# Two tiles for the weight sums of a seven-product pair, in a decoder-layer kernel

## The chip, the core and the metric

The kernel runs on one core of one Trainium2 chip, alone. Its time is the device time of one execution in microseconds, taken as the median of several executions. A profiled execution also has a span, from the start of the first instruction of the program to the end of the last.

## What is computed

One layer of a decoder with two token mixers, in float32, for 512 prompt tokens and 32 sample tokens that share the weights. Cut to the lines that lead to the weight products:

```python
h = rmsnorm(x, w['norm1']) * (1 + sc1) + sh1
bg, cg, xin, q, kc, vc, ks, vs, kw, vw, nsa_g, merge_g = split_columns(h @ w['w_in'])
v, conv_new = short_conv(cg * xin, conv_prev, w['w_conv'], w['b_conv'])
y_a = (bg * v) @ w['w_out_conv']
o_b, nsa_state = attend(qh, gates, kvh(kc, vc), kvh(ks, vs), kvh(kw, vw))
x = x + g1 * ((ga * y_a + gb * (o_b @ w['w_o_nsa'])) @ w['w_out'])
h2 = rmsnorm(x, w['norm2']) * (1 + sc2) + sh2
x = x + g2 * ((jax.nn.silu(h2 @ w['w_gate']) * (h2 @ w['w_up'])) @ w['w_down'])
```

The input projection `h @ w['w_in']` has 7,728 columns. It gives keys, values, queries, the convolution's inputs and the gates, and it is the part of the program in which the change acts.

## The kernel before, in words

**Stages.** The program runs through compressing the cached keys (lines 640 to 780), the norm and the modulation that make `h`, the input projection (lines 870 to 995), the sample group's attention beside the first part of the convolution (from line 997), the prompt's attention, the output projections, the feed-forward part (from line 1667), and the last norm. All loops are written out, and a list scheduler orders each engine's instructions when the kernel is built. On the chip each engine takes its own instructions strictly in that order, and waits at an instruction until the semaphores that it needs have come.

**A pair and its seven products.** Most of the input projection is done by `seven` (line 284). It takes 256 output columns, a "pair" of 128-column blocks, and cuts the 1,024 input rows into two halves, so that the weights are four blocks. With sums of weight blocks and sums of blocks of `h` (the tiles `S1` to `S4`), seven block products do the work of eight. The weights of a pair arrive in one tile `raw` (128 x 2048, 1 MB) as four blocks `raw[0]` to `raw[3]`. Four sums are wanted, each 128 x 512, all made by VectorE with `tensor_add`. Written with y and z for the sums, they are y1 = raw[0]+raw[3], y2 = y1+raw[1], z1 = raw[1]+raw[0], z2 = y2+raw[2].

**Operands.** A product wants its weights as two float32r tiles: ScalarE copies them into a high part (`to_hilo`, line 410, tiles `wh` or `Wh`), and VectorE subtracts that from the weights for the low part (line 411, tiles `wl` or `Wl`). Four such splits are made for each pair: W0 of raw[1:3], WY of the y sums, WZ of the z sums (128 x 1024 each), and W3 of raw[3] (128 x 512). W0 and WZ go to `wh` and `wl`, WY and W3 to `Wh` and `Wl`; each name has two buffers. A product is 12 matmuls (lines 252 to 254), so a pair is 84.

**Order inside a pair** (`wpair`, line 351). TensorE does W0's first product into `wA` and its second into `wB`, then two with WY (into `wA` and into a third accumulator `wC`), two with WZ (`wA` and `wC`), one with W3 (`wA`). After some of them ScalarE takes a copy of the accumulator, `snap` (line 301), before TensorE may go on adding into it. The outputs are put together by VectorE (`out`, lines 907 and 909) and ScalarE (line 911). The last two products of a pair come after the first one of the next pair.

**Tiles before.** y1 is written over raw[0] (line 335) and y2 over raw[1] (line 337), so WY is split from `raw`, and y2 must wait until W0's split has read raw[1]. z1 (line 334) and z2 (line 343) go to a tile `ws`, of which there are three buffers, one for each pair. `raw` has three buffers too, and the last reader of a pair's `raw` is the split W3; when it is done, SyncE starts the load for the pair three further on (line 238).

**Where pairs occur.** In the input projection there are 23 pairs, in the order of `keys`: keys and values, three of the convolution, queries, three more of the convolution, and the gates. All of them have their sums made by VectorE alone. In the feed-forward part there are 28 pairs, which are "summed": while the input projection runs, `presum` (line 558) has DMAs form y1 and z1 in DRAM, and for such a pair y1 is loaded into raw[0] and z1 into `ws` (lines 317 to 319), so VectorE makes only y2 and z2.

**Names in the profile.** The groups `ws<-raw` at line 334, `raw<-raw` at lines 335 and 337 and `ws<-raw` at line 343 are the sums. `Wl<-raw` at line 411 is WY or W3, `wl<-raw` is W0, `wl<-ws` is WZ.

Of the kernel before, what the change touches and what calls it, by code (L numbers as in the profile page):

```python
# [10 lines left out]
F32 = mybir.dt.float32  # L11
# [145 lines left out]
def build(tc, a, o):  # L157
    nc = tc.nc
    sync, act, dve, pool, pe = nc.sync, nc.scalar, nc.vector, nc.gpsimd, nc.tensor
# [14 lines left out]
    def lin_ps(nm):  # L174
        return ps.tile([128, 512], F32, tag="g", bufs=5, name=nm)
# [4 lines left out]
    def s_ps(nm):  # L180
        return ps.tile([128, 512], F32, tag="sc", bufs=2, name=nm)
# [6 lines left out]
    def nm(s):  # L188
        uid[0] += 1
        return f"{s}_{uid[0]}"  # L190
# [25 lines left out]
    def raw_tile(n):  # L216
        return wpool.tile([128, 2048], F32, tag="raw", bufs=3, name=nm(n))
# [5 lines left out]
    def queue(f, ins=lambda r: r):  # L223

        if not ordered[0]:
            return f()
        if last_q[0] is None:
            r = f()
        else:
            with tc.issue_after(last_q[0].ins):  # L230
                r = f()
        last_q[0] = ins(r)
        return r

    def slab(*key):
        nk, ncol = len(SLABS[key][1]), SLABS[key][2].shape[-1]
        v = raw_tile("raw")[:, 0:nk * ncol]
        last_slab[0] = queue(lambda: sync.dma_start(v, a["wt"][SLAB_AT[key], :, 0:nk * ncol]))
        return v.rearrange("p (k f) -> p k f", k=nk)
# [11 lines left out]
    def mm3(p, wh, wl, xh, xl, k, start, stop, **kw):  # L251
        pe.matmul(p, lhsT=wh[:, k, :], rhs=xh, start=start, stop=False, **kw)  # L252
        pe.matmul(p, lhsT=wh[:, k, :], rhs=xl, start=False, stop=False, **kw)  # L253
        pe.matmul(p, lhsT=wl[:, k, :], rhs=xh, start=False, stop=stop, **kw)  # L254
# [29 lines left out]
    def seven(o_, ww, wlp, wsp):  # L284
        wi, ns, late, later = [0], [0], [iter(())], []
        hooks = iter(o_.splits)

        def wsplit(view, odd=None):
            nk = view.shape[1]
            if odd is None:  # L290
                wi[0] += 1
                odd = wi[0] % 2
            pools = ((wpool, "wh"), (wpool, "wl")) if odd else ((ww, "Wh"), (wlp, "Wl"))
            wh, wl = (p_.tile([128, 8, 128], F32R, tag=t, bufs=2, name=nm(t))[:, 0:nk, :] for p_, t in pools)
            to_hilo(view, wh, wl)
            return wh, wl

        def snap(p):
            t = o_.snaps[ns[0] % 4]
            ns[0] += 1  # L300
            o_.snap_ops.append(act.activation(t, p, AF.Copy))  # L301
            return t

        def product(p, w, k0, X, first):
            n_ = len(X[0]) if isinstance(X[0], list) else 4
            xk = lambda t, k: t[k] if isinstance(t, list) else t[:, k, :]
            k0 *= n_
            for k in range(n_):
                mm3(p, w[0][:, k0:k0 + n_], w[1][:, k0:k0 + n_], xk(X[0], k), xk(X[1], k), k, first and k == 0, k == n_ - 1, skip_group_check=not first)

        def wslab(*key):
            n_ = len(SLABS[key][1]) // 4
            w_ = 128 * n_
            z = wsp.tile([128, 8, 128], F32, tag="ws", bufs=3, name=nm("ws"))[:, 0:2 * n_]
            if key in pre:
                v = raw_tile("raw")[:, 0:4 * w_]
                last_slab[0] = queue(lambda: sync.dma_start(v[:, w_:4 * w_], a["wt"][SLAB_AT[key], :, w_:4 * w_]))
                sync.dma_start(v[:, 0:w_], pre[key][:, w_:2 * w_])
                sync.dma_start(z[:, 0:n_].rearrange("p k f -> p (k f)"), pre[key][:, 0:w_])
            else:  # L320
                v = slab(*key).rearrange("p k f -> p (k f)")
            return v.rearrange("p (n k f) -> p n k f", n=4, k=n_), z, key in pre

        def parts(slabs):
            raw, z, summed = slabs
            n_ = raw.shape[2]
            pair = lambda i: raw[:, i:i + 2].rearrange("p n k f -> p (n k) f")
            return raw, z[:, 0:n_], z[:, n_:2 * n_], pair, summed

        def y_sums(slabs, tie=None):  # L330
            raw, z1, z2, pair, summed = parts(slabs)
            a21, a11, a12, a22 = (raw[:, i] for i in range(4))
            if not summed:
                dve.tensor_add(z1, a11, a21)
                dve.tensor_add(a21, a21, a22)
            with tc.issue_after(tie.ins) if tie else ExitStack():
                dve.tensor_add(a11, a21, a11)
            return wsplit(pair(0))

        def z_sums(slabs, tie=None):  # L340
            raw, z1, z2, pair, summed = parts(slabs)
            with tc.issue_after(tie.ins) if tie else ExitStack():
                dve.tensor_add(z2, raw[:, 1], raw[:, 2])

        def prepare(slabs):
            W0 = wsplit(parts(slabs)[3](1))
            WY = y_sums(slabs)
            z_sums(slabs)
            return W0, WY

        def wpair(slabs, out, ready=None, o_=o_, tie=None):

            W0 = wsplit(parts(slabs)[3](1)) if ready is None else ready[0]
            yield
            pA = s_ps(nm("wA"))[:, 0:WH]
            product(pA, W0, 0, o_.B11, True)
            s1 = snap(pA)
            next(late[0], None)
            pB = lin_ps(nm("wB"))[:, 0:WH]
            product(pB, W0, 1, o_.B21, True)  # L360
            out(0, 0, pB, s1)
            yield
            if ready is None:
                WY = y_sums(slabs, tie)
                z_sums(slabs, tie)
            else:
                WY = ready[1]
            WZ = wsplit(slabs[1])
            W3 = wsplit(slabs[0][:, 3])
            yield  # L370
            product(pA, WY, 1, o_.T2, False)
            s2 = snap(pA)
            for _ in late[0]:
                pass
            next(hooks, lambda: None)()
            pC = lin_ps(nm("wC"))[:, 0:WH]
            product(pC, WY, 0, o_.T1, True)
            s3 = snap(pC)
            next(hooks, lambda: None)()
            flush()  # L380
            product(pA, WZ, 0, o_.T3, False)
            out(1, 1, pA, s3)
            flush()
            next(hooks, lambda: None)()

            def rest():
                product(pC, WZ, 1, o_.B22, False)
                out(0, 1, pC, s2)
                yield
                product(pA, W3, 0, o_.T4, False)  # L390
                out(1, 0, pA, None)
                yield
            late[0] = rest()
            yield

        def flush():
            while later:
                later.pop(0)()

        def finish():  # L400
            for _ in late[0]:
                pass
            flush()
        return SimpleNamespace(wsplit=wsplit, wslab=wslab, wpair=wpair, finish=finish, later=later, prepare=prepare)

    def hcols(hf):
        return slice(*HS[hf])

    def to_hilo(src, hi, lo):
        act.activation(hi, src, AF.Copy)  # L410
        return dve.tensor_sub(lo, src, hi.bitcast(F32))  # L411
# [143 lines left out]
    pre, pre_keys, copied = {}, [(n, c2) for c2 in range(1, FC // 2) for n in ("fg", "fu")], []  # L555
# [326 lines left out]
    ready = h7.prepare(first[0])  # L882
# [682 lines left out]
    for k2 in range(4):  # L1565
# [3 lines left out]
        for kk in range(2):  # L1569
            k = k2 * 2 + kk  # L1570
# [31 lines left out]
    ws = []  # L1602
# [23 lines left out]
    for k2 in range(4):  # L1626
# [3 lines left out]
        for kk in range(2):  # L1630
            v = so[:, :, kk * 128:(kk + 1) * 128]
# [112 lines left out]
    wsplit, wslab, wpair, later = f7.wsplit, f7.wslab, f7.wpair, f7.later  # L1744
# [339 lines left out]
```

## Time and profile before

| what | value |
|---|---|
| median of 3 runs | 1204.36 us (1201.5 to 1205.96) |
| time of the profiled execution | 1200.79 us |
| its span | 1199.0 us, 1.8 us less than its time |
| TensorE (matmuls), busy | 1179.7 us, 98% |
| TensorE (weight loads), busy | 1094.4 us, 91% |
| VectorE, busy | 851.2 us, 71% |
| ScalarE, busy | 640.2 us, 53% |
| HBM traffic over the span | 235 GB/s |
| granted TensorE clock | 0.998 |

The profile is of one execution. PE is TensorE at its matmuls and PEld its weight loads, which run beside them; DVE is VectorE, ACT is ScalarE, POOL is GpSimd, SP is SyncE. A row of the timeline gives start, duration, engine, line, operation, the tile written and the tiles read, and in square brackets how long the engine was idle just before and what ended it. A row of the waits gives the engine and tile that waited, what it waited for, the total, how often, and the longest. The end of a matmul is modelled, and matmuls overlap: each is shown with some 0.29 us, while the next starts 0.13 us later. So a pause of TensorE is shorter as PE idle time than it is as time lost.

### The profile page before, as it was taken

The numbers are of one execution on the slowest core, as the hardware profiler recorded it, in microseconds if no ns is written. First come the engines' busy times: TensorE is split into PE (matmuls) and PEld (weight loads), VectorE is DVE, ScalarE is ACT, GpSimd is POOL, SyncE is SP. The second block draws the span as 40 slices with busy tenths as digits, with TensorE's granted clock in tenths as the row PEclk, the third lists the DMA queues.
The fourth block names the chain that finished last, engine by engine and source line by source line (L and its number), as shares of the span: only waits on it lengthen the run. The fifth ranks groups of instructions, "written<-read, shape, count | busy, mean of one in ns | idle before, by whom it ended". The sixth has DMA issues, their size and how long they took to land.

```text
span 1199.0 us, 25796 instructions
## 1 busy us (share of the span) xinstructions
PE 1179.7 (98%) x10114; PEld 1094.4 (91%) x10114; DVE 851.2 (71%) x1927; ACT 640.2 (53%) x1302; POOL 103.3 (9%) x154
## 2 busy tenths in 40 slices
PE   9999999999999999999999999999999999999997
PEld 7999999999999988887777778999999999999996
DVE  2539976788676477685777766667847887877776
ACT  1416544565446333386666675436645666666541
POOL 1000241000000111111101100000010001001000
PEclk9999999999999999999999999999999999999999
DMA  9963556788655998979978869545357448349412
GB/s 334 358 233 124 154 167 195 215 264 252 192 172 180 381 337 313 308 225 250 275 203 222 218 187 292 175 183 175 96 132 216 128 132 232 134 119 224 172 54 75
DMA packets 86283, 248.81 MB, mean 208 GB/s; under 512 B 9480, under 2 KB 19592, under 8 KB 74522
## 3 DMA queue, kind: packets, MB, share of 16 engines
q1 hardware_dynamic: 73330, 222.77, 53.6%
q0 software_dynamic: 12112, 23.09, 12.2%
q8 instruction: 79, 1.29, 0.4%
q10 hardware_dynamic: 720, 1.31, 0.3%
q14 instruction: 42, 0.34, 0.1%
HBM read 216.33 MB, written 65.28 MB: 235 GB/s over the span
## 4 chain that ended last, share of the span: by engine, by line
PE 76%; DMA 10%; DVE 9%; issue 2%; ACT 1%; ACTq 0%; SPq 0%; DVEq 0%; POOL 0%; POOLq 0%
DMA raw<-in_wt 8%; PE phi L674 7%; PE lin L252 7%; PE lin L253 6%; PE lin L254 6%; PE wA L254 5%; PE wA L252 5%; PE wA L253 5%; PE acc L1464 3%; PE ptp L1470 3%; PE wC L252 3%; DVE wl L411 3%; PE wC L253 3%; PE wC L254 3%; PE modp L430 2%
## 5 line engine op out<-in xcount | busy, mean ns | idle before, releaser
L410 ACT ACTIVATE Wh<-raw 128x1024 fp32r<-128x1024 f32 (+3 forms) x105 | 86.3, 823 | 78.2 <-PE wA L253 35.8
L411 DVE TENSOR_TENSOR Wl<-raw,Wh 128x1024 fp32r<-128x1024 f32 (+3 forms) x105 | 98.3, 940 | 20.3 <-ACT Wh L410 19.9
L1443 ACT ACTIVATE P<-P,nms 128x384 f32<-128x384 f32 (+3 forms) x120 | 64.9, 544 | 20.0 <-DVE nms L1442 19.3
L1442 DVE CUSTOM_DVE_ANT_0 P<-sp,ta 128x384 f32<-128x384 f32 (+3 forms) x120 | 52.1, 469 | 30.2 <-PE sp L1430 22.7
L252 PE MATMUL lin<-h_h,wh 128*128 128x288 f32 (+1 forms) x240 | 71.5, 298 | 0.0
L410 ACT ACTIVATE wh<-ws 128x1024 fp32r<-128x1024 f32 (+1 forms) x50 | 51.3, 1026 | 36.7 <-PE wC L253 20.5
L301 ACT ACTIVATE work<-wA 128x272 f32<-128x272 f32 x102 | 40.0, 392 | 56.3 <-PE wA L254 56.2
L253 PE MATMUL lin<-h_l,wh 128*128 128x288 f32 (+1 forms) x240 | 69.3, 289 | 0.0
L254 PE MATMUL lin<-h_h,wl 128*128 128x288 f32 (+1 forms) x240 | 69.1, 288 | 0.0
L411 DVE TENSOR_TENSOR wl<-raw,wh 128x1024 fp32r<-128x1024 f32 (+2 forms) x56 | 65.1, 1163 | 4.4 <-ACT wh L410 4.0
L411 DVE TENSOR_TENSOR wl<-ws,wh 128x1024 fp32r<-128x1024 f32 (+1 forms) x50 | 59.8, 1197 | 11.0 <-ACT wh L410 9.9
L247 ACT ACTIVATE wh<-raw 128x1024 fp32r<-128x1024 f32 (+1 forms) x43 | 41.9, 974 | 42.3 <-PE lin L253 25.8
L248 DVE TENSOR_TENSOR wl<-raw,wh 128x1024 fp32r<-128x1024 f32 (+1 forms) x43 | 48.3, 1123 | 21.5 <-ACT wh L247 21.3
L410 ACT ACTIVATE wh<-raw 128x1024 fp32r<-128x1024 f32 (+2 forms) x56 | 55.9, 999 | 11.5 <-PE wB L253 4.9
L674 PE MATMUL phi<-gt,wphi 128*128 128x128 f32 x512 | 61.4, 277 | 0.2 <-DMA gt<-in_cache_cmp 0.2
L674 PEld LDWEIGHTS phi<-gt,wphi 128*128 128x128 f32 x512 | 59.1, 192 | 2.4 <-issue 1.1
L573 POOL DMA_DIRECT2D pre<-in_wt x28 | 27.3, 975 | 358.4 <-DMA pre<-in_wt 358.4
L254 PE MATMUL wA<-S_hi,Wl 128*128 128x272 f32 x184 | 53.4, 290 | 1.4 <-DVE Wl L411 1.4
L252 PE MATMUL wA<-S_hi,Wh 128*128 128x272 f32 x184 | 53.4, 290 | 0.0
L253 PE MATMUL wA<-S_lo,Wh 128*128 128x272 f32 x184 | 53.1, 288 | 0.0
L252 PEld LDWEIGHTS lin<-h_h,wh 128*128 128x128 f32 x240 | 45.6, 190 | 7.5 <-issue 6.2
L665 DVE TENSOR_TENSOR xs<-gt 128x1024 f32<-128x1024 f32 x16 | 19.5, 1222 | 36.6 <-PE phi L674 20.5
(584 smaller groups left out, 4336.6 us busy)
## 6 DMA issues: line engine op xcount, KB each, us to landing
raw<-in_wt SPq DMA_DIRECT2D x68, 1024.0 KB, 6.9
raw<-in_wt SPq DMA_DIRECT2D x24, 768.0 KB, 4.8
sraw<-in_cache_sel SPq DMA_DIRECT2D x64, 256.0 KB, 5.9
gt<-in_cache_cmp SPq DMA_DIRECT2D x60, 256.0 KB, 5.7
pre<-in_wt SPq DMA_DIRECT2D x20, 512.0 KB, 8.2
pre<-in_wt POOLq DMA_DIRECT2D x20, 512.0 KB, 7.9
wraw<-in_cache_winT SPq DMA_DIRECT2D x8, 1024.0 KB, 7.9
raw<-pre SPq DMA_DIRECT2D x20, 256.0 KB, 7.4
```

Of the source, the lines that this page charges most:

```text
L247: act.activation(oh, view, AF.Copy)
L248: dve.tensor_sub(ol, view, oh.bitcast(F32))
L252: pe.matmul(p, lhsT=wh[:, k, :], rhs=xh, start=start, stop=False, **kw)
L253: pe.matmul(p, lhsT=wh[:, k, :], rhs=xl, start=False, stop=False, **kw)
L254: pe.matmul(p, lhsT=wl[:, k, :], rhs=xh, start=False, stop=stop, **kw)
L301: o_.snap_ops.append(act.activation(t, p, AF.Copy))
L410: act.activation(hi, src, AF.Copy)
L411: return dve.tensor_sub(lo, src, hi.bitcast(F32))
L674: pe.matmul(po[:, c0:c0 + 128], lhsT=w[:, ch], rhs=x[:, :, ch * 16:ch * 16 + 16], start=(n_ == 0 and ch == 0), stop=(n_ == 2 and ch == 7))
L1442: p_ops.append(dve.tensor_tensor_reduce(out=t[:, 0:n], in0=sps[br], in1=t_dist[:, 512 - n:512], scale=-hs, scalar=3e38, op0=ALU.add, op1=A ...
L1443: e_ops.append(act.activation(t[:, 0:n], t[:, 0:n], AF.Exp, scale=-1.0, bias=nms[:, c:c + 1], accum_out=sums[:, c:c + 1]))
L1464: pe.matmul(acc[br * 64:br * 64 + 64, :], lhsT=vtok[br][:, j, g * 64:(g + 1) * 64], rhs=pts_[br], start=(j == 0), stop=False)
```

## The change

For pairs whose sums VectorE makes alone, `wslab` now takes two `ws` tiles, one for y and one for z. y1 and y2 go to the first, z1 and z2 to the second, and `raw` is only read. z1 is made after WY's split is written in the program, not before. For summed pairs y stays in `raw` and z in `ws`, as before. `ws` still has three buffers, of which one unsummed pair now uses two.

```diff
             if key in pre:
+                z = sums()
                 v = raw_tile("raw")[:, 0:4 * w_]
+                y = v[:, 0:2 * w_].rearrange("p (k f) -> p k f", k=2 * n_)
...
             else:
+                y, z = sums(), sums()
                 v = slab(*key).rearrange("p k f -> p (k f)")
...
-        def y_sums(slabs, tie=None):
-            raw, z1, z2, pair, summed = parts(slabs)
-            a21, a11, a12, a22 = (raw[:, i] for i in range(4))
             if not summed:
-                dve.tensor_add(z1, a11, a21)
-                dve.tensor_add(a21, a21, a22)
+                dve.tensor_add(y[:, 0:n_], raw[:, 0], raw[:, 3])
             with tc.issue_after(tie.ins) if tie else ExitStack():
-                dve.tensor_add(a11, a21, a11)
-            return wsplit(pair(0))
+                dve.tensor_add(y[:, n_:2 * n_], y[:, 0:n_], raw[:, 1])
+            return wsplit(y)

         def z_sums(slabs, tie=None):
-            raw, z1, z2, pair, summed = parts(slabs)
+            raw, y, z, summed = slabs
+            n_ = raw.shape[2]
+            if not summed:
+                dve.tensor_add(z[:, 0:n_], raw[:, 1], raw[:, 0])
             with tc.issue_after(tie.ins) if tie else ExitStack():
-                dve.tensor_add(z2, raw[:, 1], raw[:, 2])
+                dve.tensor_add(z[:, n_:2 * n_], y[:, n_:2 * n_], raw[:, 2])
```

The new lines: y1 is line 334, y2 line 336, z1 line 343, z2 line 345. Everything below the functions moves down by two lines: the splits are at 412 and 413, the outputs at 909, 911 and 913. Each tile has a number that differs between the two programs.

VectorE in the eighteenth of the 23 pairs, which stands for all from the fourth on. Before, raw_451 is pair 17, raw_464 pair 18 and raw_478 pair 19 (the first is pair 0); ws_450 and ws_463 hold the z sums of 17 and 18.

```order
L334 TENSOR_TENSOR ws_477_4012<-raw_478_4013 128x512
L411 TENSOR_TENSOR wl_460_3883<-ws_450_3771,wh_459_3882 128x1024
L907 TENSOR_TENSOR work7_1595<-wB_456_3860,work7_1595 128x272
L411 TENSOR_TENSOR wl_466_3894<-raw_464_3891,wh_465_3893 128x1024
L335 TENSOR_TENSOR raw_478_4013<-raw_478_4013 128x512
L337 TENSOR_TENSOR raw_464_3891<-raw_464_3891 128x512
L411 TENSOR_TENSOR Wl_462_3887<-raw_451_3772,Wh_461_3886 128x512
L343 TENSOR_TENSOR ws_463_3890<-raw_464_3891 128x512
L411 TENSOR_TENSOR Wl_472_4000<-raw_464_3891,Wh_471_3999 128x1024
L909 SCALAR_TENSOR_TENSOR work7_1595<-wA_455_3833,work7_1595 128x272
L907 TENSOR_TENSOR work7_1595<-wC_467_3923,work7_1595 128x272
```

The same place after. raw_469, raw_483 and raw_498 are pairs 17, 18 and 19; ws_468 is the z tile of 17, ws_481 the y tile of 18, ws_496 and ws_497 the y and z tiles of 19.

```order
L413 TENSOR_TENSOR wl_478_3901<-ws_468_3789,wh_477_3900 128x1024
L909 TENSOR_TENSOR work7_1596<-wB_474_3878,work7_1596 128x272
L413 TENSOR_TENSOR wl_485_3913<-raw_483_3910,wh_484_3912 128x1024
L334 TENSOR_TENSOR ws_496_4031<-raw_498_4033 128x512
L336 TENSOR_TENSOR ws_496_4031<-ws_496_4031,raw_498_4033 128x512
L413 TENSOR_TENSOR Wl_480_3905<-raw_469_3790,Wh_479_3904 128x512
L413 TENSOR_TENSOR Wl_491_4018<-ws_481_3908,Wh_490_4017 128x1024
L911 SCALAR_TENSOR_TENSOR work7_1596<-wA_473_3851,work7_1596 128x272
L343 TENSOR_TENSOR ws_497_4032<-raw_498_4033 128x512
L345 TENSOR_TENSOR ws_497_4032<-ws_496_4031,raw_498_4033 128x512
L909 TENSOR_TENSOR work7_1596<-wC_486_3942,work7_1596 128x272
```

The first instruction that reads pair 19's `raw` stood ahead of the low parts of WZ of 17 and of W0 of 18; now it stands behind both. y2 and z2 of pair 18 stood between W0 of 18 and WY of 18; now all four sums of a pair are made a pair earlier, and the sums in this stretch are those of pair 19. TensorE's and ScalarE's order is the same in both programs from pair 2 on, but for one place: in the pair of 230 us ScalarE's snap of `wA` now stands ahead of its copy of W3.

ScalarE at the start of the stage. Before, raw_179 is pair 0, raw_195 pair 1, raw_184 the operand sums S3 and S4, and `wA_187` pair 0's accumulator.

```order
L410 ACTIVATE Wh_192_1641<-raw_179_1521 128x512
L410 ACTIVATE S4_hi_1509<-raw_184_1535 128x1088
L301 ACTIVATE work7_1595<-wA_187_1597 128x272
L410 ACTIVATE wh_190_1637<-ws_178_1520 128x1024
L410 ACTIVATE wh_196_1648<-raw_195_1646 128x1024
L301 ACTIVATE work7_1595<-wA_187_1597 128x272
```

The same place after, with raw_180 for pair 0, raw_197 for pair 1, raw_185 for the operand sums and `wA_188` for the accumulator.

```order
L412 ACTIVATE Wh_193_1642<-raw_180_1522 128x512
L412 ACTIVATE wh_191_1638<-ws_179_1521 128x1024
L412 ACTIVATE wh_198_1650<-raw_197_1648 128x1024
L412 ACTIVATE S4_hi_1509<-raw_185_1536 128x1088
L301 ACTIVATE work7_1596<-wA_188_1598 128x272
L301 ACTIVATE work7_1596<-wC_200_1667 128x272
L301 ACTIVATE work7_1596<-wA_188_1598 128x272
```

Two weight copies moved ahead of S4 and of the first snap of `wA`. On VectorE the two low parts that belong to WY and WZ of pair 0 moved ahead of the last subtraction that makes S4 (line 742, now 744), and so did one more of the sums. On TensorE pair 0's product into `wC` was cut in two by its product into `wA`; now it runs whole, with four matmuls of pair 1, ahead of it.

More of the change, by code (lines that the diff above doesn't have):

```diff
@@ L313, in wslab @@
             w_ = 128 * n_
-            z = wsp.tile([128, 8, 128], F32, tag="ws", bufs=3, name=nm("ws"))[:, 0:2 * n_]
+            sums = lambda: wsp.tile([128, 8, 128], F32, tag="ws", bufs=3, name=nm("ws"))[:, 0:2 * n_]
             if key in pre:
+                z = sums()
                 v = raw_tile("raw")[:, 0:4 * w_]
+                y = v[:, 0:2 * w_].rearrange("p (k f) -> p k f", k=2 * n_)
                 last_slab[0] = queue(lambda: sync.dma_start(v[:, w_:4 * w_], a["wt"][SLAB_AT[key], :, w_:4 * w_]))
@@ L320, in wslab, with first_tile, y_sums @@
             else:
+                y, z = sums(), sums()
                 v = slab(*key).rearrange("p k f -> p (k f)")
-            return v.rearrange("p (n k f) -> p n k f", n=4, k=n_), z, key in pre
-        def parts(slabs):
-            raw, z, summed = slabs
-            n_ = raw.shape[2]
-            pair = lambda i: raw[:, i:i + 2].rearrange("p n k f -> p (n k) f")
-            return raw, z[:, 0:n_], z[:, n_:2 * n_], pair, summed
-        def y_sums(slabs, tie=None):
-            raw, z1, z2, pair, summed = parts(slabs)
-            a21, a11, a12, a22 = (raw[:, i] for i in range(4))
+            return v.rearrange("p (n k f) -> p n k f", n=4, k=n_), y, z, key in pre
+        def first_tile(slabs):
+            return wsplit(slabs[0][:, 1:3].rearrange("p n k f -> p (n k) f"))
+        def y_sums(slabs, tie=None):
+            raw, y, z, summed = slabs
+            n_ = raw.shape[2]
             if not summed:
-                dve.tensor_add(z1, a11, a21)
-                dve.tensor_add(a21, a21, a22)
+                dve.tensor_add(y[:, 0:n_], raw[:, 0], raw[:, 3])
             with tc.issue_after(tie.ins) if tie else ExitStack():
-                dve.tensor_add(a11, a21, a11)
-            return wsplit(pair(0))
+                dve.tensor_add(y[:, n_:2 * n_], y[:, 0:n_], raw[:, 1])
+            return wsplit(y)
         def z_sums(slabs, tie=None):
-            raw, z1, z2, pair, summed = parts(slabs)
+            raw, y, z, summed = slabs
+            n_ = raw.shape[2]
+            if not summed:
+                dve.tensor_add(z[:, 0:n_], raw[:, 1], raw[:, 0])
             with tc.issue_after(tie.ins) if tie else ExitStack():
-                dve.tensor_add(z2, raw[:, 1], raw[:, 2])
+                dve.tensor_add(z[:, n_:2 * n_], y[:, n_:2 * n_], raw[:, 2])
         def prepare(slabs):
-            W0 = wsplit(parts(slabs)[3](1))
+            W0 = first_tile(slabs)
             WY = y_sums(slabs)
@@ L351, in wpair @@
         def wpair(slabs, out, ready=None, o_=o_, tie=None):
-            W0 = wsplit(parts(slabs)[3](1)) if ready is None else ready[0]
+            W0 = first_tile(slabs) if ready is None else ready[0]
             yield
@@ L367, in wpair @@
                 WY = ready[1]
-            WZ = wsplit(slabs[1])
+            WZ = wsplit(slabs[2])
             W3 = wsplit(slabs[0][:, 3])
```

## The prediction

> **What bounds the kernel now.** I read the page's engine table first, then the busy time by stretch, then the waits of the stretch in which the change acts, then the timeline around single stops of TensorE.
>
> ```profile
> span 1199.0 us, 25796 instructions
> PE 1179.7 (98%) x10114; PEld 1094.4 (91%) x10114; DVE 851.2 (71%) x1927; ACT 640.2 (53%) x1302; POOL 103.3 (9%) x154
> ```
>
> TensorE bounds the program. Whatever the change does to VectorE counts only where TensorE stops, and in the whole program it is idle for 1199.0 − 1179.7 = 19.3 us. The input projection's pairs run from 122 to 390 us. Each row gives a window and its length, then busy time and number of instructions for PE, PEld, DVE, ACT and POOL, then granted clock, DMA share and GB/s.
>
> ```profile
> 122.00:390.00 268.00, 261.86 (x2097) 258.77 (x2096) 203.98 (x301) 142.54 (x221) 31.50 (x35) 1.00 0.67 201
> ...
> 240.00:300.00 60.00, 60.00 (x480) 59.98 (x480) 51.44 (x87) 36.12 (x56) 1.76 (x2) 1.00 0.82 258
> ...
> 390.00:400.00 10.00, 10.00 (x93) 9.78 (x92) 3.25 (x13) 5.12 (x10) 0.13 (x2) 1.00 0.99 357
> ```
>
> TensorE idles 268.00 − 261.86 = 6.1 us here, and none of it between 240 and 300 us. There 480 matmuls take 60.00 us, 0.125 us each, so a pair of 84 takes 10.5 us. What the other stretches wait for, by the waits of 122 to 390 us (total, times, longest):
>
> ```profile
> DVE ws L334 <- DMA raw<-in_wt: 35.5, 14, 6.5
> ACT Wh L410 <- DVE raw L337: 26.6, 15, 3.4
> PEld wC L252 <- ACT work L301: 4.2, 6, 1.3
> PEld wA L252 <- ACT work L301: 2.1, 1, 2.1
> PEld wA L254 <- DVE Wl L411: 1.8, 2, 1.2
> ```
>
> The weight loads waited 4.2 + 2.1 + 1.8 = 8.1 us in 9 stops. The matmuls' idle time of 6.1 us is less than the loss, because a matmul is drawn with 0.39 us where its operands are new while its successor could start 0.125 us after it: some 0.2 us more for each stop, 7.9 us. I take 8.1 us as what can be won. The timeline of one stop shows how the first two rows lead to the third.
>
> ```profile
> 331.84 0.69 DVE L334 TENSOR_TENSOR ws<-raw 128x512 f32<-128x512 f32 x1 [3.66 <-DMA raw<-in_wt]
> 332.45 1.22 DVE L411 TENSOR_TENSOR wl<-ws,wh 128x1024 fp32r<-128x1024 f32 x1
> 333.59 0.43 DVE L907 TENSOR_TENSOR work<-wB,work 128x272 f32<-128x272 f32 x1
> 333.94 1.22 DVE L411 TENSOR_TENSOR wl<-raw,wh 128x1024 fp32r<-128x1024 f32 x1
> 335.07 0.69 DVE L335 TENSOR_TENSOR raw<-raw 128x512 f32<-128x512 f32 x1
> 335.68 0.69 DVE L337 TENSOR_TENSOR raw<-raw 128x512 f32<-128x512 f32 x1
> 336.28 0.69 DVE L411 TENSOR_TENSOR Wl<-raw,Wh 128x512 fp32r<-128x512 f32 x1
> ...
> 336.48 1.06 ACT L410 ACTIVATE Wh<-raw 128x1024 fp32r<-128x1024 f32 x1 [3.36 <-DVE raw L337]
> 337.44 0.38 ACT L301 ACTIVATE work<-wC 128x272 f32<-128x272 f32 x1
> 337.87 0.39 PE L252 MATMUL wC<-h_h,wh 128*128 128x272 f32 x1 [1.10 <-ACT work L301]
> ```
>
> VectorE idles 3.66 us for a transfer that only L334 needs, a sum for the pair after next. The low parts of the pair at hand wait behind it. Then y2 (L337) is late, ScalarE's copy of the y sums waits for it 3.36 us, the snap of `wC` stands behind that copy, and TensorE waits 1.10 us for the snap.
>
> **Part 1: the loads leave the path (23 pairs).** The change makes as many sums as before and as many splits, so VectorE's work is equal: 4 sums of 0.6 us and 4 splits a pair. What moves is the place of the first reader of a load. Before, a load that starts when W3 is done must be followed, before the next W3 is done, by L334 (0.61 us to the next row), WZ (1.14), the output (0.35), W0 (1.13), two sums (0.61 + 0.60) and W3 (0.69): 5.1 us. In a period of 10.5 us a load may take 5.4 us. After, only two sums and W3 follow it: 1.9 us, so a load may take 8.6 us. Loads, on the chain of waits (start and duration):
>
> ```profile
> 162.33 8.70 DMA raw<-in_wt
> ...
> 280.74 9.18 DMA raw<-in_wt
> ...
> 336.99 4.67 DMA raw<-in_wt
> ```
>
> They lie between 4.7 and 9.2 us, so most fit in 8.6 us and few in 5.4. The 0.6 us by which the longest overrun are covered: above, W3's low part is done at 336.97, and TensorE needs it after the 12 matmuls that start at 337.87 and 8 more, at 340.4: 3.4 us of slack. Also, the four sums of a pair are now made a pair early, so ScalarE's copy of the y sums finds them ready, and the snap behind it comes in time. The `wC` stops (4.2) and the `Wl` stops (1.8: a low part in the same queue behind L334) should go. What is late next is W3, by nothing that reaches TensorE.
>
> The longest single stop is another branch of the same tree:
>
> ```profile
> 230.54 0.69 DVE L334 TENSOR_TENSOR ws<-raw 128x512 f32<-128x512 f32 x1 [2.53 <-DMA raw<-in_wt]
> ...
> 233.23 0.40 DVE L199 COPY rows<-sps 32x256 f32<-32x256 f32 x1
> 233.66 1.91 ACT L840 ACTIVATE vext<-rows 32x2048 f32<-32x2048 f32 x1 [3.01 <-DVE rows L199]
> 236.57 0.39 PE L252 MATMUL wA<-S_hi,wh 128*128 128x272 f32 x1 [1.90 <-ACT work L301]
> ```
>
> ScalarE's `vext` waits for a copy that VectorE can only make after its 2.53 us behind L334. Without that wait the copy is 2.5 us earlier, against a stop of 2.1 us. The margin of 0.4 us is the thinnest of all: between none and all of 2.1 us can stay. I count it as gone and hold a reserve below.
>
> **Part 2: the start of the stage gets worse.** The order shows ScalarE's copy into `S4_hi` and pair 0's first snap of `wA` behind two weight copies, because on VectorE one more sum and two 128x1024 low parts stand ahead of the subtraction that makes S4 (its high part is `S_hi<-raw` in the rows).
>
> ```profile
> 130.06 1.28 DVE L742 TENSOR_TENSOR raw<-raw,xT 128x1088 f32<-128x1088 f32 x1
> 131.66 1.10 ACT L410 ACTIVATE S_hi<-raw 128x1088 fp32r<-128x1088 f32 x1
> 132.66 0.37 ACT L301 ACTIVATE work<-wA 128x272 f32<-128x272 f32 x1
> 132.82 0.39 PE L252 MATMUL wC<-S_hi,Wh 128*128 128x272 f32 x1
> ```
>
> By the durations above, L742 comes 0.61 + 2 x 1.13 = 2.9 us later, so `S4_hi` starts at 134.5 and the snap, 1.00 us behind it as in the rows, at 135.5. TensorE can go on 0.43 us later (337.44 to 337.87 above), at 135.9. It has 12 matmuls of `wC` and 4 of the next pair ahead of what needs the snap: from 132.82, 16 x 0.125 = 2.0 us, until 134.9. It waits 1.0 us. The bounds are 0, if VectorE reaches the subtraction earlier by a gap that I don't count, and 2.9, if none of the 16 matmuls covers any of it. I take 1.0, which the rows count out.
>
> **Part 3: more sums beside GpSimd.** One more sum now falls in the stretch after 143 us, where GpSimd copies.
>
> ```profile
> 143.33 9.89 POOL L817 COPY x<-work 64x256 f32<-64x256 f32 x8
> L334 DVE TENSOR_TENSOR ws<-raw x23: 681/692/1120, 125.8 to 363.3; 128x512 f32<-128x512 f32 x23
> ```
>
> The slowest of the 23 sums took 1120 ns against a median of 692, so 0.43 us is what one sum loses at most by the rows; it is in the reserve. The Trainium skill ("SBUF — State Buffer", section "Who interferes with whom") goes further: an operation of VectorE with two inputs in SBUF and one of GpSimd that reads SBUF exclude each other, the later one being blocked outright. By that rule the sum could wait for a whole copy of 9.89 / 8 = 1.24 us, and the gain would be estimated at 0.8 us less; the row of 1120 ns shows contention but no such block.
>
> Other edits: y2 no longer overwrites raw[1], so it needn't wait for W0's split, which stands ahead of it anyway: nothing. `ws` takes two of its three buffers per pair; y of pair p+2 reuses z of pair p, read last by WZ(p), which VectorE has behind it when it comes to that sum: nothing. From 390 us on both programs are the same.
>
> **The sum.** 8.1 − 1.0 = 7.1 us. The reserve for the near ties (0.4 us at `vext`, 0.43 beside GpSimd) is 0.8: 6.3 us. The profiled execution took 1200.79 us, 1.8 outside its span; it would take 1194.5. It was 3.6 us under the median of the runs, so against that: 1204.36 − 6.3 = 1198.1 us. The ends of this case are −8.1 (nothing lost at the start) and 8.1 − 2.9 − 2.1 − 0.43, a gain of 2.7 (all lost there, `vext` keeping its stop): 1196.3 to 1201.7.
>
> **Rivals.** First, the gain is given back behind the stage. From 390 us the row above shows a DMA share of 0.99 and 357 GB/s. If the transfers there limit TensorE, coming 6.3 us earlier only means waiting longer: half back gives 1201.2, all 1204.4. Against it speaks that TensorE is busy 10.00 of 10 us there; and where the DMA share is 0.82 (240 to 300 us), 60.00 of 60. For it speaks that with `raw` freed no earlier than W3 and TensorE going faster, loads lengthen with the share.
>
> Second, slower. All loads of `raw`, by the page (number, size, median us from issue to landing):
>
> ```profile
> raw<-in_wt SPq DMA_DIRECT2D x68, 1024.0 KB, 6.9
> ```
>
> The load now stands ahead of W3 and of WY of the next pair, so a late one closes a loop, W3, load, two sums, W3, that no later step makes good. It decides from a mean load of 8.6 us. At 9.6 us, 20 pairs lose 1.0 us each; less 3.4 of slack and 7.1 of gain, that is +9.5: 1213.9 us. For it: the longest above take 8.7 and 9.2 us, and TensorE's faster pace asks for more bandwidth. Against it: their median is 6.9, and from 240 to 300 us, where the share is 0.82 and a load from 280.74 takes 9.18 us, TensorE had no stop.
>
> The Trainium skill ("Perfetto Trace Analysis", section "Optimization Strategy") says that the same gap coming back on the engine that should be saturated can mean too few buffers for the next tile. This change gives a pair two buffers of three, so by the rule gaps would come back; no run here shows it so far, and VectorE's order speaks against it.
>
> **How the numbers follow.** The forecast case gets 0.64, the first rival 0.28, the second 0.08. Two kernels of this time can be told apart by about 0.5%, 6.0 us here, so the bound is 1198.3. The forecast lies just beyond it; a little over half of its case, 0.38, counts as faster, and 0.26 as the same. With the first rival and 0.02 of the second, same has 0.56; slower has 0.06. The range goes from 1196.3 less 1.8 (the runs of before lie 2.9 under and 1.6 over their median, a median of such less) to the first rival's end plus 0.6: 1194.5 to 1205.0. It leaves out the second rival and little more.
>
> **What would show it.** Right: in 122 to 390 us TensorE idle under 2 us, the waits of `Wh` for the y sums near zero, the waits of the first sum for loads far under 35.5 us, and one stop of 1.0 us near 135 us with the snap as its releaser. Wrong: stops of similar sum with W3 or WY as releaser (second rival), a shorter stage but an equal span (first rival), the 2.1 us still at `vext`, or loads of over 8.6 us in the mean.

## The result, and the profile after

The median fell by 10.8 us, from 1204.36 to 1193.57 us (seven executions each). The ratio on record, over all fourteen, is 0.9916 with an interval of 0.9894 to 0.9938; the medians alone divide to 0.9910. The forecast was 1198.1, and the range ended at 1194.5: the direction was right, the gain larger than it held. A second measurement of the same two kernels gave 0.9935 (0.9917 to 0.9954), with 8.7 us between the medians (1203.15 and 1194.46).

The profiled execution took 1191.61 us. Its page, and the windows of the stage (window, length, busy time and instructions of PE, PEld, DVE, ACT and POOL, clock, DMA share, GB/s):

```profile
span 1189.8 us, 25820 instructions
PE 1177.5 (99%) x10114; PEld 1094.1 (92%) x10114; DVE 854.2 (72%) x1927; ACT 641.0 (54%) x1302; POOL 103.8 (9%) x154
```

```profile
122.00:390.00 268.00, 267.40 (x2168) 265.87 (x2168) 208.83 (x304) 147.06 (x227) 32.15 (x37) 1.00 0.69 211
122.00:166.00 44.00, 43.41 (x348) 42.54 (x349) 43.22 (x56) 24.38 (x37) 19.29 (x19) 1.00 0.57 172
166.00:240.00 74.00, 74.00 (x617) 73.52 (x616) 54.60 (x82) 38.22 (x59) 6.04 (x8) 1.00 0.72 222
240.00:300.00 60.00, 60.00 (x481) 59.98 (x480) 51.84 (x86) 35.69 (x56) 2.64 (x3) 1.00 0.80 233
300.00:390.00 90.00, 90.00 (x730) 89.83 (x728) 59.17 (x81) 48.77 (x75) 4.17 (x8) 1.00 0.64 205
```

The same stretches of before in which TensorE stopped:

```profile
122.00:166.00 44.00, 42.61 (x337) 41.34 (x336) 41.64 (x53) 23.92 (x37) 20.09 (x20) 1.00 0.59 167
166.00:240.00 74.00, 71.13 (x589) 69.99 (x589) 50.02 (x77) 35.76 (x57) 4.74 (x6) 1.00 0.67 198
300.00:390.00 90.00, 88.12 (x697) 87.46 (x696) 60.88 (x86) 46.73 (x74) 4.91 (x7) 1.00 0.61 182
```

TensorE's idle time in the stage fell from 6.1 to 0.6 us, and what is left lies ahead of 166 us. The waits of 122 to 390 us (total, times, longest) that answer to those of before:

```profile
DVE ws L334 <- DMA raw<-in_wt: 4.9, 3, 2.6
ACT Wh L412 <- DVE ws L336: 1.4, 1, 1.4
PEld wA L252 <- ACT work L301: 1.0, 2, 0.8
PE wA L252 <- ACT work L301: 0.6, 1, 0.6
ACT vext L842 <- DVE rows L199: 0.4, 1, 0.4
```

VectorE's waits for loads fell from 35.5 to 4.9 us, ScalarE's for y2 from 26.6 to 1.4, and the stops behind snaps of `wC` are gone. One stop is left (beside one of 0.2 us right behind it), the new one at the start. It comes about as forecast, with the subtraction for S4 2.5 us later than before where 2.9 was reckoned:

```profile
132.60 1.28 DVE L744 TENSOR_TENSOR raw<-raw,xT 128x1088 f32<-128x1088 f32 x1
...
133.91 1.11 ACT L412 ACTIVATE S_hi<-raw 128x1088 fp32r<-128x1088 f32 x1 [1.31 <-DVE raw L744]
...
134.93 0.38 ACT L301 ACTIVATE work<-wA 128x272 f32<-128x272 f32 x1
...
135.37 0.39 PE L252 MATMUL wA<-S_hi,Wh 128*128 128x272 f32 x1 [0.59 <-ACT work L301]
```

The place that was shown at 331 to 338 us comes next. WZ's low part, which started at 332.45 us, now starts at 322.78:

```profile
322.78 1.23 DVE L413 TENSOR_TENSOR wl<-ws,wh 128x1024 fp32r<-128x1024 f32 x1 [0.52 <-ACT wh L412]
323.92 0.43 DVE L909 TENSOR_TENSOR work<-wB,work 128x272 f32<-128x272 f32 x1
324.29 1.22 DVE L413 TENSOR_TENSOR wl<-raw,wh 128x1024 fp32r<-128x1024 f32 x1
325.43 0.69 DVE L334 TENSOR_TENSOR ws<-raw 128x512 f32<-128x512 f32 x1
326.15 0.69 DVE L336 TENSOR_TENSOR ws<-ws,raw 128x512 f32<-128x512 f32 x1
326.87 0.69 DVE L413 TENSOR_TENSOR Wl<-raw,Wh 128x512 fp32r<-128x512 f32 x1
328.81 1.23 DVE L413 TENSOR_TENSOR Wl<-ws,Wh 128x1024 fp32r<-128x1024 f32 x1 [1.25 <-ACT Wh L412]
```

No row here waits for a load. In the stage VectorE's idle time now goes mostly to waits for ScalarE's copies and for TensorE.

**Where the time went.** The first matmul of the compressed keys and the first of the sample group's scores have the same work between them in both programs. Their rows, of before and then of after:

```profile
12.92 0.46 PE L674 MATMUL phi<-gt,wphi 128*128 128x128 f32 x2 [0.25 <-DMA gt<-in_cache_cmp]
...
409.46 1.07 PE L1183 MATMUL ss<-sraw,qbd 128*32 128x512 f32 x8
```

```profile
12.67 0.72 PE L676 MATMUL phi<-gt,wphi 128*128 128x128 f32 x5
...
401.58 1.06 PE L1185 MATMUL ss<-sraw,qbd 128*32 128x512 f32 x8
```

396.54 us against 388.91. Below, "stage" is this distance, and "rest" runs from the first score matmul to the start of the last matmul; both are from the profiled execution.

| kernel | that execution, us | stage | rest | ratio to before (interval) |
|---|---|---|---|---|
| before | 1200.79 | 396.54 | 781.6 | |
| b_again, b_third | 1198.81, 1202.56 | 395.88, 397.90 | 780.2, 782.1 | 1.0001 (0.9986 to 1.0015), none |
| after | 1191.61 | 388.91 | 780.3 | 0.9916 (0.9894 to 0.9938) |
| a_again, a_third | 1192.11, 1192.61 | 389.02, 388.91 | 780.4, 781.0 | 0.9935 (0.9917 to 0.9954), none |
| order_alone | 1195.64 | 389.63 | 783.2 | 0.9934 (0.9916 to 0.9952) |
| before_two_ws | 1195.40 | 390.47 | 782.1 | 0.9949 (0.9931 to 0.9968) |
| y_tile_alone | 1210.10 | 405.98 | 781.5 | 1.0041 (1.0024 to 1.0059) |
| before_w3_early | 1199.54 | 396.68 | 780.1 | 1.0000 (0.9986 to 1.0014) |
| y_tile_w3_early | 1201.79 | 394.93 | 784.1 | 0.9996 (0.9983 to 1.0008) |
| after_two_ws | 1194.37 | 389.26 | 782.5 | 0.9927 (0.9911 to 0.9944) |
| after_s4_first | 1194.16 | 388.22 | 783.3 | 0.9918 (0.9899 to 0.9937) |
| after_s4_first_two_ws | 1192.08 | 389.18 | 780.2 | 0.9923 (0.9904 to 0.9943) |
| before_longer_loads | 1212.25 | 407.90 | 781.8 | 1.0068 (1.0047 to 1.0090) |
| after_longer_loads | 1203.16 | 399.44 | 781.0 | 1.0039 (1.0023 to 1.0054) |
| after_long_loads | 1217.83 | 414.98 | 780.3 | 1.0159 (1.0134 to 1.0184) |

### The profile page after: what moved, and what is told of

The parts are those of the page before. It is cut to its first block, busy times and chain, and to the rows that moved or that the text cites. A ratio compares the mean times of both kernels' runs of the same rounds, so it can differ in the third digit from the quotient of the medians.

```text
span 1189.8 us, 25820 instructions
## 1 busy us (share of the span) xinstructions
PE 1177.5 (99%) x10114; PEld 1094.1 (92%) x10114; DVE 854.2 (72%) x1927; ACT 641.0 (54%) x1302; POOL 103.8 (9%) x154
## 4 chain that ended last, share of the span: by engine, by line
PE 92%; DVE 4%; DMA 2%; ACT 1%; issue 1%; POOL 0%; DVEq 0%; ACTq 0%; POOLq 0%
PE wA L254 8%; PE wA L252 8%; PE wA L253 8%; PE phi L676 7%; PE lin L252 7%; PE lin L253 7%; PE lin L254 7%; PE wC L253 4%; PE wC L254 4%; PE wC L252 4%; PE acc L1466 3%; PE ptp L1472 3%; PE modp L432 2%; PE wB L252 2%; PE wB L254 2%; PE wB L253 2%
## 5 line engine op out<-in xcount | busy, mean ns | idle before, releaser
L412 ACT ACTIVATE Wh<-raw 128x1024 fp32r<-128x1024 f32 (+2 forms) x82 | 62.1, 757 | 49.7 <-PE wA L253 34.9
L413 DVE TENSOR_TENSOR Wl<-raw,Wh 128x1024 fp32r<-128x1024 f32 (+2 forms) x82 | 70.1, 855 | 21.9 <-ACT Wh L412 21.4
L412 ACT ACTIVATE wh<-raw 128x1024 fp32r<-128x1024 f32 (+2 forms) x56 | 56.1, 1001 | 12.6 <-PE wB L253 5.1
L253 PEld LDWEIGHTS lin<-h_l,wh 128*128 128x128 f32 x240 | 45.2, 188 | 0.1
```

## The experiments

The theory was that a wait for a load stands ahead of low parts that TensorE needs soon, and that its place in VectorE's queue is what counts. Its rival was that y in its own tile counts, since y2 then needn't follow W0's split. The diffs below are shortened: conditions are left out, and plain names stand for the instructions that are waited for.

**Order alone, tiles alone.** The first keeps before's tiles and only holds the first two sums back:

```diff
+            with tc.issue_after(z2_of_the_pair_before.ins):
                 dve.tensor_add(z1, a11, a21)
                 dve.tensor_add(a21, a21, a22)
```

> Before's tiles (y over raw, three z tiles), with z1 and y1 of a pair held behind z2 of the pair before in VectorE's order. Theory (a wait for a load stands ahead of the low parts; where it stands is what counts): nearly all is gained, 6 to 10 us, ratio 0.9915 to 0.995, and the waits of Wh for y2 and the stops behind snaps of wC fall under 1 us. Rival (y2 written over raw must wait for W0's split, and its own tile is what frees it): under 2 us gained, ratio 0.998 to 1.001, waits of Wh for y2 still above 15 us.

The second starts from the kernel after. It gives y its own tile, one of three for each pair, and writes z over raw:

```diff
-                y, z = sums(), sums()
+                y = sums()
                 v = slab(*key).rearrange("p k f -> p (k f)")
+                z = v[:, 0:2 * w_].rearrange("p (k f) -> p k f", k=2 * n_)
```

> y in a tile of its own (one of three for each pair), z written over raw, so that the first sum of a load stands ahead of WZ's low part as in before, while the y sums of a pair are made a pair early as in after. Theory: VectorE still waits some 30 us for loads ahead of the low parts; stops behind wl, Wl and the vext copy stay (3 to 5 us), the snaps of wC no longer wait behind the y copy; 3 to 6 us gained, ratio 0.995 to 0.9975. Rival (tiles are all): the whole gain, ratio 0.990 to 0.993. Rival (order is all): no gain, 0.998 to 1.002.

Holding the sums back gave 0.9934, as much as the change in the same measurement (0.9935). The tile alone gave 1.0041: slower. Its waits for loads and what TensorE waited for:

```profile
DVE ws L335 <- DMA raw<-in_wt: 52.7, 15, 5.6
PEld wA L254 <- DVE wl L414: 10.1, 8, 3.2
PEld wA L252 <- ACT work L301: 3.9, 3, 3.1
ACT vext L843 <- DVE rows L199: 3.6, 1, 3.6
```

and those of the order alone:

```profile
ACT Wh L412 <- DVE raw L339: 5.0, 4, 2.8
PEld wA L254 <- DVE Wl L413: 1.1, 1, 1.1
DVE ws L336 <- DMA raw<-in_wt: 0.9, 1, 0.9
PEld wC L252 <- ACT work L302: 0.2, 1, 0.2
```

The waits of ScalarE's copies for y2 stayed at 5.0 us with the order alone, where under 1 was expected, and cost TensorE no stop of over 0.2 us behind a snap of `wC`. So the order is the cause, and the tiles matter because they bring it about. The rival that tiles are all falls. So does the theory's figure for y's own tile, 3 to 6 us gained: early y sums did end the stops behind snaps of `wC`, but stops behind `wl` took their place and more, and the ring has one sum more in it. The ring is the prediction's loop: W3 done, load, first sum, and what VectorE does from there up to the next W3.

**Ring or queue?** Two readings were left. In the ring reading only the length of load plus VectorE's work up to W3 counts, against a pair's 10.5 us. In the blocking reading it counts whose low parts stand behind the wait. W3's low part was put right behind W0's, so that the ring is 1.2 us shorter while the same low parts wait:

```diff
-                dve.tensor_add(a21, a21, a22)
+                with tc.issue_after(W3_low_two_pairs_back.ins):
+                    dve.tensor_add(a21, a21, a22)
...
+            with tc.issue_after(W3_low_of_the_pair_before.ins):
                 dve.tensor_add(a11, a21, a11)
```

> The kernel before, with W3's low part put ahead of the sums y1 and y2 that stood between W0's low part and it; the first sum (line 336 here), which waits for the load, still stands ahead of WZ's and W0's low parts. Loop theory (what costs is the length of the ring W3, load, first sum, ..., W3 against a pair's 10.5 us; the part on VectorE shrinks from 5.15 to 4.0 us): 4 to 8 us gained, ratio 0.9935 to 0.997, stops of TensorE in the stage 2 to 5 us. Blocking theory (what costs is whose low parts stand behind the wait): no gain or a loss, ratio 0.998 to 1.003, since the same low parts wait and y2 is 0.6 us later.

The ratio was 1.0000, so the ring reading falls for before. The stops behind snaps went, as with y's own tile, and stops behind low parts came. TensorE and VectorE at one of them, in order of time:

```profile
288.06 0.29 PE L253 MATMUL wA<-S_lo,wh 128*128 128x272 f32 x1
...
288.65 0.69 DVE L336 TENSOR_TENSOR ws<-raw 128x512 f32<-128x512 f32 x1 [4.21 <-DMA raw<-in_wt]
289.26 1.22 DVE L415 TENSOR_TENSOR wl<-ws,wh 128x1024 fp32r<-128x1024 f32 x1
...
290.53 0.51 PE L254 MATMUL wA<-S_hi,wl 128*128 128x272 f32 x1 [2.19 <-DVE wl L415]
```

The low part of WZ starts 0.6 us after a sum that it doesn't need, and TensorE stands 2.19 us for it: blocking, in the rows. The same edit on the kernel with y's own tile (z sums and y2 held behind W3):

> The kernel with y in its own tile and z over raw, and W3's low part ahead of the three sums that stood before it, so that the ring's part on VectorE shrinks from 5.75 to 4.0 us. Loop theory: the 5 us lost turn into a gain, ratio 0.990 to 0.9965, some 9 to 14 us better than with W3 behind the sums. Blocking theory: still 1.000 or more, stops behind wl of 8 us or more.

It gave 0.9996, in the stage 405.98 to 394.93 us. Here the ring did count, for 11 us of the stage, but only back to about before's level. Each reading forecast another ratio or larger stops behind `wl` (they sum to 5 us): neither alone holds.

**The low parts freed by one number.**

```diff
-            z = wsp.tile([128, 8, 128], F32, tag="ws", bufs=3, ...
+            z = wsp.tile([128, 8, 128], F32, tag="ws", bufs=2, ...
```

> The kernel before with two ws buffers in place of three: z1 of a pair must now come after WZ of the pair two before, and the scheduler puts it behind W0's low part too, but still ahead of y2 and of W3. Low-part theory (a wait for a load ahead of WZ's and W0's low parts is what reaches TensorE): 5 to 8 us gained, ratio 0.9935 to 0.997, though y2 and the copy of the y sums still stand behind the wait. Copy theory (y2 late, ScalarE's copy of the y sums late, the snap of wC behind it): 0 to 3 us gained, stops behind snaps of wC of 3 us or more.

0.9949: the low-part theory holds, the copy theory falls. ScalarE still waits 10.9 us for y2, but no stop of over 0.2 us behind a snap of `wC` comes of it. What is left are two `Wl` stops at the start:

```profile
ACT Wh L410 <- DVE raw L337: 10.9, 7, 3.0
DVE ws L334 <- DMA raw<-in_wt: 8.8, 6, 2.4
PEld wA L254 <- DVE Wl L411: 2.2, 2, 1.5
PEld wC L252 <- ACT work L301: 0.2, 1, 0.2
```

With the third buffer z1 may be made early, so it is put where its wait does harm; without it z1 must follow WZ's split. That also shortens the ring by the 2.6 us of the two low parts and the output between them, so the shares of ring and blocking were not separated: every order that frees the low parts does both.

The change itself with two buffers. The rival here is the rule of the Trainium skill ("Perfetto Trace Analysis", section "Optimization Strategy") that a gap which keeps coming back can mean too few buffers:

> The kernel after with two ws buffers in place of three, so that the y sums of a pair come after WY of the pair before, and z after its WZ. Theory (what counts is that no wait for a load stands ahead of low parts that TensorE needs; the loads have more time here): within 2 us of after, ratio 0.990 to 0.995. Rival (too few buffers make the same gap come back in each pair): 5 us or more slower than after, ratio over 0.996.

0.9927, and beside the one at 135 us no stop of over 0.2 us. What the skill's rule warns of is shown by no run here; before itself got faster when its third buffer was taken away.

**Longer loads.** The load is issued in two parts, with a copy inside DRAM between them (0:1536 of it in the third kernel):

```diff
-                v = slab(*key).rearrange("p k f -> p (k f)")
...
+                r = queue(lambda: sync.dma_start(v[:, 0:512], src[:, 0:512]))
...
+                    r = sync.dma_start(xx, src[:, 0:512])
...
+                    last_slab[0] = last_q[0] = sync.dma_start(v[:, 512:2048], src[:, 512:2048])
```

> The kernel before, with each of the 23 loads of raw issued as a quarter, then a copy of 0.25 MB inside DRAM that nothing reads, then the other three quarters, so that it lands later. Theory (a loop W3, load, first sum, two low parts, W3 binds from loads of 5.4 us): loads grow from about 6.5 to 8 us, and each further us costs nearly 1 us per pair: 15 to 35 us longer than before. Rival (loads are hidden, and the stops come from the queue of ScalarE alone): under 5 us longer.

> The kernel after with the same longer loads. Theory (its loop binds from 8.6 us): 0 to 6 us longer than after, so 20 us or more under before with the same loads. Rival (the traffic itself slows the program): both grow alike.

> The kernel after with a copy of 0.75 MB inside DRAM between the parts of each load. Theory: loads of 10 to 12 us are past 8.6 us, and the loop W3, load, two sums, W3 now stops TensorE in each pair: 20 to 60 us longer than after, the stops with W3's or WY's low part (Wl) or the snap behind it as releaser. This is the second rival of the prediction, reached on purpose. If it costs under 10 us, the bound of 8.6 us is wrong.

The stage grew by 11 us in before, by 10.5 in after, by 26 with the larger copy. After's profiled execution is the shortest of its kernel; by the medians the whole program grew by 9 us in before (1203.06 to 1212.06) and by 13 in after (1194.46 to 1207.1). That after would lose less was wrong: its loads got longer than I had reckoned, past 8.6 us. One turn of after's ring, VectorE's and SyncE's rows in order of time:

```profile
296.34 0.68 DVE L419 TENSOR_TENSOR Wl<-raw,Wh 128x512 fp32r<-128x512 f32 x1
297.05 0.33 SPq L326 DMA_DIRECT2D raw<-in_wt  x1
298.64 0.60 SPq L330 DMA_DIRECT2D raw<-in_wt  x1
305.79 0.69 DVE L340 TENSOR_TENSOR ws<-raw 128x512 f32<-128x512 f32 x1 [2.05 <-DMA raw<-in_wt]
306.51 0.69 DVE L342 TENSOR_TENSOR ws<-ws,raw 128x512 f32<-128x512 f32 x1
307.12 0.68 DVE L419 TENSOR_TENSOR Wl<-raw,Wh 128x512 fp32r<-128x512 f32 x1
307.83 0.33 SPq L326 DMA_DIRECT2D raw<-in_wt  x1
```

8.7 us from issue to landing, 2.0 to the next issue: 10.8 us against a pair's 10.5. The 12 loads on which VectorE waited for over 0.7 us took 6.6 to 12.6 us from the first issue to landing, 9.5 in the mean, so that the ring stops TensorE. This is the prediction's second rival, reached on purpose. The totals by themselves also fit the rival that the traffic slows both kernels alike; that the loss goes through the ring rests on the rows, and on the stops of the kernel with the larger copy, most of which have `Wl` as releaser. Before's kernel is no fair partner: with the longer loads the scheduler put its first sums behind the low parts of its own accord (y2, y1 and W3 follow them directly in its rows).

**The new stop removed.** `sum_3()` and `sum_4()` are written ahead of `h7.prepare(first[0])`:

> The kernel after, with S3 and S4 written in the program ahead of the first pair's sums, so that S4 and the first snap come as early as before. Theory: the stop of 0.88 us near 135 us goes, 0.5 to 1.0 us less than after in the stage, ratio 0.990 to 0.994. Rival: the stop moves to the first Wl parts at 142 to 155 us, as in before (1 to 2 us), and nothing is gained.

> The same with two ws buffers. Theory: as the one with three within 1 us, 0.990 to 0.994, 4 KB per partition saved. Rival (fewer buffers bring gaps back): over 0.995.

With three buffers the stop at 135 us is gone and the stage takes 388.22 us, 0.7 less than after; in the whole program 0.9918 is not apart from after. With two, a stop of 0.9 us at 153 us comes instead (389.18), and the ratio is 0.9923. Nothing beat the change by what can be measured.

**How far executions differ.**

> The kernel before, unchanged, to learn how far two executions of it differ and where. Theory (the stops of TensorE in 122 to 390 us come from the timing of loads, which changes from one execution to the next): the stops there again sum to 6 to 11 us but not at the same places, the rest of the program agrees within 1 us with the first profile, ratio to itself 0.998 to 1.002. Rival (the time that after gained outside the stage is the change's too): the small stops near 652, 746 and 929 us of the first profile come back, each within 0.2 us.

> The kernel after, unchanged. Theory: one stop of 0.6 to 0.9 us near 135 us and under 1 us of others in the stage; against a second profile of before the stage is 7 to 10 us shorter; ratio 0.990 to 0.993. Rival (the first measurement was lucky, and the forecast of 6.3 us was right): ratio 0.994 to 0.996.

> The kernel before, a third profile. Theory (the gain is the stage's alone): from the first phi matmul to the first of the sample scores 396 us again within 1 us, what follows varies by up to 4 us with no relation to the change. Rival (before's stage itself varies, and its slower executions lose there): 398 us or more in the stage when the execution is slow.

> The kernel after, a third profile. Theory: 389 us within 0.5 us in the stage, and the rest as in before, 780 to 784 us. Rival (the change also shortens what follows): under 779 us there, below all profiles of before.

The stage of after varied by 0.1 us, that of before by 2.0, and the longest of its three executions has the longest stage. Outside the stage all kernels lie between 780.1 and 784.1 us without relation to the change: the small stops of before at 652 and 746 us are not in b_again but come back in b_third, and that at 929 us is in all three and in a_again and a_third too. Four of these expectations were missed by a little. The rest of b_again differs from before's by 1.3 us, not by under 1. The stage of a_again is 6.9 us shorter than that of b_again, not 7 to 10, and its ratio of 0.9935 lies between the theory's range and the rival's. The stage of b_third took 397.9 us, not 396 within 1, and so nearly what the rival said, that before's slower executions lose there.

## Why the prediction was wrong, point by point

- **What bounds it** was right: matmul by matmul, the gain comes in eight steps of 0.5 to 2.1 us, each where TensorE had stopped.
- **Part 1** was right in mechanism. All stops but the new one went: 7.63 us of net gain in the profiled pair plus 0.75 (0.88 less one pitch of 0.13) for the new stop makes 8.4, where 8.1 was forecast. The stops at 145 and 155 us (the `Wl` row, 1.8 us) were laid to the wrong cause: no wait for a load stands there, since VectorE works without a pause from 139.7 to 156 us in before, beside GpSimd's copies for most of it. One such stop stays with order_alone and with after_s4_first_two_ws, both stay with before_two_ws, none with after. Why none stays there is not shown. Of the stop of 2.1 us at 236.57, up to 0.54 us may be ScalarE's own: in after, in order_alone and in before_two_ws its snap of `wA` no longer stands behind its copy of W3 there. In after the snap of `wC` also stands behind the copy of the y sums there and again in the pair of 367 us, so ScalarE's order differs in more than the one place named above.
- **Part 2**: 1.0 us forecast, 0.75 measured.
- **Part 3 and the reserve failed as a size.** 0.8 us was held back, and none was lost. `vext` waits 0.4 us for VectorE without stopping TensorE. Beside GpSimd a sum lost 0.43 us, as forecast, but one subtraction lost 1.02 us; TensorE lost nothing by it (last section).
- **The step that failed is the low end of the range, in how the numbers follow.** It allowed a gain of 9.9 us: 8.1 for the stops, with nothing lost at the start, and 1.8 for the scatter of medians. The stops' term held: the stage gained 7.63 us. The term that was too small is the 1.8. Of the 10.8 us, 0.25 are at the program's start and 1.3 in the rest, where executions differ by up to 4 us; and before's profiled execution was 3.6 us under its median, after's 2.0 under its, which makes another 1.6. That is 3.1 us outside the stops of the profiled pair. The forecast itself lost another 0.8 by the reserve, which nothing called for. That the 3.1 us are chance is argued, not shown. For it speaks that the second measurement gave 8.7 us, which the low end allows. Against it, the stops of one execution are not a fixed sum: the weight loads' waits come to 8.1, 7.4 and 9.2 us in the three profiles of before, whose stages are 7.6, 7.0 and 9.0 us longer than after's 388.9. Before's executions of 1204 us and more were not profiled, and may lose more in the stage.
- **The first rival** (given back behind the stage) fell: the rest is the same. **The second** was not reached by the change, but the kernels made for it stopped as it says once loads took over 8.6 us; how exact that bound is was not measured.

## What to carry to other kernels

In an engine that takes its instructions in order, the first reader of a transfer belongs behind everything that the bound engine needs soon, even when it could be put earlier; look for what follows each instruction that waits for a DMA. A spare buffer can do harm, since it lets a scheduler put that reader early, and one buffer less can be nearly as good as a rewrite. Price such stops from several executions, for they change from one to the next.

## What the runs showed of the hardware

GpSimd's copies slow VectorE's sums and subtractions beside them, and are slowed by them. VectorE's rows of after beside them, GpSimd's, and one copy of before with no VectorE instruction beside it:

```profile
143.60 1.22 DVE L413 TENSOR_TENSOR wl<-ws,wh 128x1024 fp32r<-128x1024 f32 x1
144.73 2.24 DVE L413 TENSOR_TENSOR wl<-raw,wh 128x1024 fp32r<-128x1024 f32 x1
146.90 1.11 DVE L336 TENSOR_TENSOR ws<-ws,raw 128x512 f32<-128x512 f32 x1
147.94 1.11 DVE L413 TENSOR_TENSOR Wl<-raw,Wh 128x512 fp32r<-128x512 f32 x1
148.97 1.12 DVE L343 TENSOR_TENSOR ws<-raw 128x512 f32<-128x512 f32 x1
```

```profile
144.88 9.38 POOL L819 COPY x<-work 64x256 f32<-64x256 f32 x8
```

```profile
165.09 0.62 POOL L817 COPY x<-work 64x256 f32<-64x256 f32 x1
```

A 128x1024 subtraction took 2.24 us in place of 1.22, a loss of 1.02 us in one instruction, and each 128x512 operation 1.11 in place of 0.69. A copy took 1.17 us in the mean, where the one by itself took 0.62. The Trainium skill ("SBUF — State Buffer", section "Who interferes with whom") says that a VectorE instruction with two inputs in SBUF contends with a GpSimd one that reads SBUF, and that the port pair they share is an exclusive lock. That both sides are slowed agrees with it. A block for the whole of each instruction does not quite come out of the rows: a sum (0.60 us to the next row) and a copy (0.62) in turn would take 1.22 us, an estimate from these rows, and the 128x512 operations start every 1.04 us.
